# Row blocks of a mixture-of-experts layer rounded up to multiples of 16

## The chip, the cores and the metric

The kernel runs on one core of a Trainium2 chip. The metric is the device time of one execution in microseconds (us); the time of a kernel is the median of several runs.

## The reference

One layer of a hybrid encoder, for 1024 tokens of width 1024: a token mixer, and then a mixture of experts, which is where the change lies. Cut to that:

```python
logits = hf @ router_w + router_b                     # 32 experts
top_logits, top_idx = lax.top_k(logits, 4)
gates = softmax(top_logits)
...
def expert(xb, e):
    up = xb @ w_up[e] + b_up[e]                       # 1024 -> 2048
    x_glu, x_lin = split(up, 2)
    x_glu = minimum(x_glu, 7.0); x_lin = clip(x_lin, -7.0, 7.0)
    act = x_glu * sigmoid(1.702 * x_glu) * (x_lin + 1.0)
    return act @ w_down[e] + b_down[e]                # 1024 -> 1024
...
y[t] = sum over the 4 experts of gates[t, k] * expert(h[t], top_idx[t, k])
out = rms_norm(x + g2 * y, final_norm_w)
```

Each token's result is the gated sum over its four experts; a row that is added with a value of zero changes nothing.

## The kernel before, in words

Until about 585 us the token mixer and the router run. They leave in HBM the normalised tokens `h2s` (1024 rows of 2048 float16 values: high and low halves of each number), the residual `acc_d` (1024 float32 rows) to which the experts add, and a table `idtab`, which holds for each expert the list of its tokens (row number and gate). The 128 rows behind row 1024 of `h2s`, `acc_d` and `out` are zeros, and unused entries of the table point at them.

Then 32 experts follow. They are ranked by their load, and the expert of rank r is given room for `CAPS[r]` tokens (210, 192, 182 down to 108). `ORDER` pairs a small one with a large one: ranks 29, 0, 28, 1, 27, 2 and so on, and at the end 30 and 31. For an expert with room for n tokens (class `Expert`, L1699):

- The list is cut into blocks of up to 128 rows (`self.rows`, L1703): 210 becomes 128 + 82, 114 stays one block of 114. There are 52 blocks with 4522 rows in all.
- `load_ids` (L1714) reads a block's piece of the table. `gather` (L1726) has GpSimd (POOL) fetch the block's rows of `h2s` into the tile `xr` by an indirect DMA. `turn_x` (L1734) transposes them on TensorE (PE) into `xT`, with ScalarE copying out of PSUM.
- Three kinds of phases follow: G and L (the two halves of the up projection) and D (the down projection). Experts with more than 170 rows have them in halves. In a phase PE multiplies 128x128 pieces of weights, each three times (high and low halves), by all n columns (L1787 to L1789).
- The weights come as float32 in pieces of 512 KB into 14 buffers `wf`, by DMAs that SP issues (L1766). ScalarE and VectorE split each piece into float16 halves `wh` and `wl` (L1886, L1887), up to six pieces ahead of the matmuls.
- What a phase leaves in PSUM is worked on during the next phase, in slots between its matmuls (`epilogue`). For G that is a clamp on VectorE, a sigmoid on ScalarE and a product on POOL (L1810, the gate product). For D, `y_pieces` (L1848) has ScalarE write `yT` (feature by token, one buffer), PE transposes it back block by block (L1872), ScalarE scales by the gates into `yr` (L1873), and POOL adds the rows to `acc_d` by an indirect DMA that accumulates (L1875). That scatter waits for the landing of the scatter before it.

So the work of POOL is in program order: gate products, table pieces, gathers for the expert two places later (slot 5 of a phase), scatters. The last expert does not scatter: `LastRows.gather` and `finish` (L1960, L1966) fetch its rows of `acc_d`, add, normalise and write them to `out`, after `FinalNorm` has loaded, normalised (the pairs L1948 and L1949 on POOL) and stored all other rows.

Of the kernel before, what the change touches and what calls it, by code (L numbers as in the profile page):

```python
# [11 lines left out]
F32 = mybir.dt.float32  # L12
# [3 lines left out]
AF = mybir.ActivationFunctionType  # L16
# [107 lines left out]
def build(ctx, tc, A, out, dbg=None):  # L124
    nc = tc.nc
    V, S, G, PE, SY = nc.vector, nc.scalar, nc.gpsimd, nc.tensor, nc.sync
# [8 lines left out]
    def pst(shape=(128, 512), dt=F32, tag="g"):  # L135
        return ps.tile(list(shape), dt, name=f"ps_{tag}", bufs=BANKS[tag])
# [11 lines left out]
    id16 = cst.tile([128, 128], F16, name="id16")  # L148
# [105 lines left out]
    for r0, src in ((0, A["b_mod"]), (48, A["c"]), (56, A["norm1_w"]), (64, A["norm2_w"])):  # L254
        n = src.shape[1] // 128
# [62 lines left out]
    p = pst(tag="o")  # L318
# [909 lines left out]
    for i in range(-1, NT):  # L1228
        h = i + 1
        n = 2 if left["s5"] else 1  # L1230
# [358 lines left out]
    t, b, i = NT - 3, NT - 2, NT - 1  # L1589
# [36 lines left out]
    mx = mctx.enter_context(tc.tile_pool(name="mx", bufs=2))  # L1626

    def tpt(shape=(128, 512), dt=F32):
        return tpp.tile(list(shape), dt, name="tp")
# [3 lines left out]
    with tc.manual_schedule():  # L1633
# [6 lines left out]
        p = tpt()  # L1640
# [15 lines left out]
        p = tpt()  # L1656
# [15 lines left out]
        g2s = mc.tile([128, 8], F32, name="g2s")  # L1672
# [26 lines left out]
    class Expert:  # L1699
        def __init__(self, n, e, row, bias, q, tail=False):  # L1700
            self.n, self.get_e, self.get_row, self.bias, self.q = n, e, row, bias, q
            self.eid = None
            self.rows = [(0, min(n, 128))] + ([(128, n - 128)] if n > 128 else [])  # L1703
            self.per = 512 // n
            every, lo, hi = list(range(8)), [0, 1, 2, 3], [4, 5, 6, 7]
            fits = 3 * self.per >= 8
            self.down = [every] if fits else [lo, hi]
            if fits and not tail:
                self.up = [[("G", every)], [("L", every)]]
            else:  # L1710
                self.up = [[("G", lo), ("L", lo)], [("G", hi), ("L", hi)]]
            self.xT = self.aT = self.yT = self.glu = self.final = None

        def load_ids(self, after=(), q=None):  # L1714
            self.ids = []
            q = q or self.q
            row = self.get_row(q)
            for j, (r0, c) in enumerate(self.rows):
                t = mx.tile([c, 2], I32, name=f"ids{j}", bufs=7)
                ld = q.dma_start(t, idtab[ds(row + r0, c), :])  # L1720
                for s in after:
                    tc.add_manual_dep(ld.ins, s.ins.name, mybir.DependencyInfo(mybir.DependencyClass.Sync, mybir.DependencyReason.DATA),
                                      reason="every entry of the table")
                self.ids.append(t)

        def gather(self):  # L1726
            self.xr = []
            for j, (r0, c) in enumerate(self.rows):
                x = mx.tile([c, 2 * D], F16, name=f"xr{j}", bufs=2)
                G.indirect_dma_start(out=x, out_offset=None, in_=h2s[:, :],  # L1730
                                     in_offset=bass.IndirectOffsetOnAxis(ap=self.ids[j][:, 0:1], axis=0))
                self.xr.append(x)

        def turn_x(self):  # L1734
            def piece(j, q):
                r0, c = self.rows[j]
                if self.xT is None:
                    self.xT = mx.tile([128, 16, self.n], F16, name="xT")
                p = tpt((128, 8, c), F16)
                for k in range(8):  # L1740
                    kk_ = q * 8 + k
                    PE.transpose(p[:, k, :], self.xr[j][:, kk_ * 128:(kk_ + 1) * 128], id16[0:c, 0:c])  # L1742
                S.copy(self.xT[:, q * 8:q * 8 + 8, r0:r0 + c], p)  # L1743

            return [(0 + 2 * j + q, lambda j=j, q=q: piece(j, q)) for j in range(len(self.rows)) for q in range(2)]
# [6 lines left out]
    class Phase:  # L1752
# [95 lines left out]
        def y_pieces(self):  # L1848
            x = self.x
            if x.yT is None:  # L1850
                x.yT = mx.tile([128, 8, x.n], F32, name="yT", bufs=1)

            def evac(q):
                for i, m in enumerate(self.ms):
                    b = i // x.per
                    if b // 2 != q:
                        continue
                    S.activation(x.yT[:, m, :], self.loc(i), AF.Identity, scale=g2s[:, m:m + 1], bias=x.bias(16 + m))  # L1858

            ps_ = [(q, lambda q=q: evac(q)) for q in range(2)]  # L1860
            if self.ms[-1] != 7:
                return ps_
            yr = {}

            def rows(j, q):
                r0, c = x.rows[j]
                if q == 0:
                    yr[j] = mx.tile([c, D], F32, name=f"yr{j}", bufs=1)
                y = yr[j]
                p = tpt()  # L1870
                for m in range(4):
                    PE.transpose(p[0:c, m * 128:(m + 1) * 128], x.yT[:, q * 4 + m, r0:r0 + c], ident)  # L1872
                S.activation(y[:, q * 512:(q + 1) * 512], p[0:c, :], AF.Copy, scale=x.ids[j][:, 1:2].bitcast(F32))  # L1873
                if q == 1:
                    G.indirect_dma_start(out=acc_d[:, :],  # L1875
                                         out_offset=bass.IndirectOffsetOnAxis(ap=x.ids[j][:, 0:1], axis=0),
                                         in_=y, in_offset=None, compute_op=ADD)

            if x.final:
                return ps_ + [(3, lambda: x.final(x))]  # L1880
            return ps_ + [(3 + 2 * j + q, lambda j=j, q=q: rows(j, q)) for j in range(len(x.rows)) for q in range(2)]

    def split_w(w):
# [73 lines left out]
    class LastRows:  # L1957


        def gather(self, x):  # L1960
            c = x.n
            self.x = stg.tile([128, D], F32, name="wf")[0:c, :]
            G.indirect_dma_start(out=self.x, out_offset=None, in_=acc_d[:, :],
                                 in_offset=bass.IndirectOffsetOnAxis(ap=x.ids[0][:, 0:1], axis=0))

        def finish(self, x):  # L1966
            c = x.n
            ids = x.ids[0]
            z = stg.tile([128, D], F32, name="wf")[0:c, :]
            junk = mx.tile([128, D], F32, name="yr1", bufs=1)  # L1970
            y = self.y = mx.tile([c, D], F32, name="ly", bufs=1)
            ss = mx.tile([128, 2], F32, name="ls", bufs=1)[0:c, :]
            for q in range(2):
                p = tpt()
                cs = slice(q * 512, (q + 1) * 512)
                for m in range(4):
                    PE.transpose(p[0:c, m * 128:(m + 1) * 128], x.yT[:, q * 4 + m, :], ident)
                V.scalar_tensor_tensor(y[:, cs], p[0:c, :], ids[:, 1:2].bitcast(F32), self.x[:, cs], op0=MULT, op1=ADD)
                S.activation(junk[0:c, cs], y[:, cs], AF.Square, accum_out=ss[:, q:q + 1])
            G.tensor_scalar(ss[:, 0:1], ss[:, 0:1], 1.0 / D, EPS, op0=MULT, op1=ADD)  # L1980
            G.tensor_scalar(ss[:, 0:1], ss[:, 1:2], 1.0 / D, ss[:, 0:1], op0=MULT, op1=ADD)
            G.tensor_tensor(ss[:, 0:1], ss[:, 0:1], mhalf[0:c, 0:1], op=OP.pow)
            for q in range(2):
                cs = slice(q * 512, (q + 1) * 512)
                V.scalar_tensor_tensor(z[:, cs], y[:, cs], ss[:, 0:1], fw[0:c, cs], op0=MULT, op1=MULT)
            G.indirect_dma_start(out=out[:, :], out_offset=bass.IndirectOffsetOnAxis(ap=ids[:, 0:1], axis=0),
                                 in_=z, in_offset=None)
# [46 lines left out]
    with tc.If(over > 0):  # L2034
# [15 lines left out]
        for q in range(4):  # L2050
            p = tpt()
# [5 lines left out]
        p = tpt()  # L2057
# [5 lines left out]
        with tc.For_i(0, over, 1) as bi:  # L2063
# [5 lines left out]
            x = Expert(128, lambda: e, lambda q: row, lambda m: bt[:, m:m + 1], SY, True)  # L2069
# [37 lines left out]
```

## Time and profile before

| | |
|---|---|
| time, median of 3 runs | 1909.22 us (1908.97 to 1916.93) |
| the profiled execution | 1911.87 us, its span 1910.2 us |
| PE busy | 1753.9 us, 92% of the span |
| VectorE (DVE) busy | 1583.3 us, 83% |
| ScalarE (ACT) busy | 1236.3 us, 65% |
| GpSimd (POOL) busy | 575.1 us, 30% |
| indirect gathers L1730, scatters L1875 | 52 and 51 |

The profile is one execution. PE's matmuls overlap, so that its busy time says that it has work, not that it is at its peak. "Clock" is the share of full speed that TensorE was granted. A wait is put down to what ended last before the waiting instruction could start. "Us to landing" of a DMA runs from its issue to the time at which its last data has arrived.

### The profile page before, as it was taken

To read this page: it belongs to the slowest core of one execution; us is meant where nothing else is said; L and a number is where in the kernel's file an instruction comes from. 1 tells how busy PE (TensorE), PEld (TensorE's weight loads), DVE (VectorE), ACT (ScalarE), POOL (GpSimd) and SP (SyncE) were. 2 spreads that over 40 slices of the span, in tenths; PEclk is the share of its full clock that TensorE was granted. 3 is DMA by queue.
4 is the path that set the end of the run, shared out by engine and by line. 5 is a ranking of instruction groups with operands and counts; after the bars stand their busy time and mean duration, and the time that the engine had idled before them with its cause. 6 is when DMAs were issued, how large, how long until landed. Compare 5 with 4: busy or idle time off the path is not lost.

```text
span 1910.2 us, 57330 instructions
## 1 busy us (share of the span) xinstructions
PE 1753.9 (92%) x23174; PEld 1559.7 (82%) x23174; DVE 1583.3 (83%) x2430; ACT 1236.3 (65%) x1714; POOL 575.1 (30%) x505
## 2 busy tenths in 40 slices
PE   6889988999974999999999989999999999999983
PEld 3756665556643899999999979999999999999973
DVE  7858677765576888888897969999999999999985
ACT  2722333212234777777787868888888888888874
POOL 3834110143434223132221413213133333233214
PEclk9989999999996999999999989999999999999997
DMA  8841246632229999999998989999999999999996
GB/s 293 285 103 39 59 148 201 215 128 71 72 81 287 335 317 288 355 327 336 329 346 285 365 268 380 368 367 372 361 371 355 366 365 341 369 374 354 364 327 206
DMA packets 189451, 533.54 MB, mean 279 GB/s; under 512 B 37710, under 2 KB 47880, under 8 KB 189148
## 3 DMA queue, kind: packets, MB, share of 16 engines
q1 hardware_dynamic: 167548, 490.92, 71.6%
q0 software_dynamic: 21344, 37.85, 8.3%
q8 instruction: 183, 3.00, 0.6%
q10 hardware_dynamic: 288, 1.05, 0.1%
q14 instruction: 88, 0.72, 0.1%
HBM read 489.81 MB, written 39.30 MB: 277 GB/s over the span
## 4 chain that ended last, share of the span: by engine, by line
PE 46%; DMA 12%; ACT 4%; DVE 3%; issue 3%; POOL 1%; SPq 0%; DVEq 0%; ACTq 0%; POOLq 0%
PE ac L1787 14%; PE ac L1788 14%; PE ac L1789 14%; DMA wf<-in_w_up_dram 10%; ACT wh L1886 3%; DVE wl L1887 2%; PE tp L1872 2%; PE tp L1742 2%; DMA wf<-in_w_down_dram 2%; DMA xr<-h2s,ids 1%; ACT yT L1858 1%; POOL fs L1948 0%; ACT yr L1873 0%; DMA idtab<-pairs,dest 0%; POOL fs L1949 0%
## 5 line engine op out<-in xcount | busy, mean ns | idle before, releaser
L1887 DVE SCALAR_TENSOR_TENSOR wl<-wf,wh 128x1024 f16<-128x1024 f32 x768 | 944.5, 1270 | 137.3 <-ACT wh L1886 127.5
L1886 ACT ACTIVATE wh<-wf 128x1024 f16<-128x1024 f32 x768 | 774.3, 1055 | 50.3 <-DMA wf<-in_w_up_dram 21.4
L1789 PE MATMUL ac<-xT,wl 128*128 128x122 f16 (+27 forms) x4096 | 770.3, 226 | 4.5 <-DVE wl L1887 4.5
L1787 PE MATMUL ac<-xT,wh 128*128 128x122 f16 (+27 forms) x4096 | 770.9, 226 | 3.2 <-DVE el L1826 1.4
L1788 PE MATMUL ac<-xT,wh 128*128 128x122 f16 (+27 forms) x4096 | 770.4, 226 | 0.6 <-ACT xT L1743 0.6
L1789 PEld LDWEIGHTS <-wl 128*128 128x128 f16 x6144 | 602.2, 98 | 10.9 <-DVE wl L1887 8.8
L1788 PEld LDWEIGHTS <-wh 128*128 128x128 f16 x6144 | 603.4, 98 | 5.5 <-issue 4.1
L1787 PEld LDWEIGHTS <-wh 128*128 128x128 f16 x6144 | 602.9, 98 | 5.5 <-ACT wh L1886 3.6
L1787 PE MATMUL ac<-aT,wh 128*128 128x122 f16 (+27 forms) x2048 | 380.0, 226 | 3.1 <-DVE eg L1804 2.0
L1789 PE MATMUL ac<-aT,wl 128*128 128x122 f16 (+27 forms) x2048 | 380.0, 225 | 1.8 <-DVE wl L1887 1.7
L1788 PE MATMUL ac<-aT,wh 128*128 128x122 f16 (+27 forms) x2048 | 380.0, 225 | 0.9 <-DVE aT L1840 0.9
L1875 POOL DMA_INDIRECT acc_d<-yr,ids x51 | 135.2, 2651 | 592.2 <-ACT yr L1873 409.0
L1810 POOL TENSOR_TENSOR eg<-eg,es 128x420 f32<-128x420 f32 (+28 forms) x74 | 102.5, 1385 | 301.7 <-ACT es L1809 301.7
L1858 ACT ACTIVATE yT<-ac,BALL,g2s 128x122 f32<-128x122 f32 (+27 forms) x256 | 97.7, 473 | 9.1 <-PE ac L1789 9.1
L1837 ACT ACTIVATE aT<-el 128x420 f16<-128x420 f32 (+28 forms) x74 | 45.2, 611 | 90.2 <-DVE el L1830 89.3
L1743 ACT COPY xT<-tp 128x1024 f16<-128x1024 f16 (+27 forms) x104 | 75.8, 730 | 29.9 <-PE tp L1742 29.5
L1730 POOL DMA_INDIRECT xr<-h2s,ids x52 | 85.7, 1647 | 30.8 <-issue 19.7
L1809 ACT ACTIVATE es<-eg 128x420 f32<-128x420 f32 (+28 forms) x74 | 44.8, 605 | 74.3 <-DVE eg L1804 72.2
L1742 PE MATMUL tp<-id,xr 128*128 128x128 f16 (+27 forms) x832 | 54.3, 204 | 29.6 <-DMA wf<-in_w_up_dram 22.8
L1872 PE MATMUL tp<-C,yT 128*128 128x128 f32 (+27 forms) x408 | 68.4, 281 | 13.4 <-ACT yT L1858 10.1
L1826 DVE TENSOR_SCALAR el<-ac,BALL 128x122 f32<-128x122 f32 (+27 forms) x256 | 75.9, 355 | 0.0
L1804 DVE TENSOR_SCALAR eg<-ac,BALL 128x122 f32<-128x122 f32 (+27 forms) x256 | 74.8, 355 | 0.0
(495 smaller groups left out, 2426.0 us busy)
## 6 DMA issues: line engine op xcount, KB each, us to landing
wf<-in_w_up_dram SPq DMA_DIRECT2D x512, 512.0 KB, 8.4
wf<-in_w_down_dram SPq DMA_DIRECT2D x256, 512.0 KB, 10.0
wst<-in_w_mod_dram SPq DMA_DIRECT2D x40, 512.0 KB, 4.4
wst<-in_w_in_dram SPq DMA_DIRECT2D x16, 576.0 KB, 5.5
x<-in_x_dram SPq DMA_DIRECT2D x16, 512.0 KB, 4.4
hTb<-hT_d SPq DMA_DIRECT2D x16, 512.0 KB, 5.4
wA<-in_w_mod_dram SPq DMA_DIRECT2D x8, 512.0 KB, 10.3
hT_d<-hTa SPq DMA_DIRECT2D x8, 512.0 KB, 5.5
```

The costliest lines, as they stand in the source:

```text
L1730: G.indirect_dma_start(out=x, out_offset=None, in_=h2s[:, :], in_offset=bass.IndirectOffsetOnAxis(ap=self.ids[j][:, 0:1], axis=0))
L1742: PE.transpose(p[:, k, :], self.xr[j][:, kk_ * 128:(kk_ + 1) * 128], id16[0:c, 0:c])
L1787: PE.matmul(dst, h[:, ms], xh, start=k == 0 and m % x.per == 0, stop=False, skip_group_check=True)
L1788: PE.matmul(dst, h[:, ms], xl, start=False, stop=False, skip_group_check=True)
L1789: PE.matmul(dst, l[:, ms], xh, start=False, stop=k == 7, skip_group_check=True)
L1810: G.tensor_tensor(g, g, s, op=MULT)
L1826: V.tensor_scalar(t[i][:, q, :], self.loc(i + q), x.bias(8 + m), 8.0 * SS, op0=ADD, op1=MIN)
L1858: S.activation(x.yT[:, m, :], self.loc(i), AF.Identity, scale=g2s[:, m:m + 1], bias=x.bias(16 + m))
L1872: PE.transpose(p[0:c, m * 128:(m + 1) * 128], x.yT[:, q * 4 + m, r0:r0 + c], ident)
L1875: G.indirect_dma_start(out=acc_d[:, :], out_offset=bass.IndirectOffsetOnAxis(ap=x.ids[j][:, 0:1], axis=0), in_=y, in_offset=None, compute_ ...
L1886: S.activation(h, w, AF.Copy, scale=SW)
L1887: V.scalar_tensor_tensor(l, w, SW, h, op0=MULT, op1=SUB)
```

## The change

`self.rows` becomes a list of triples: first row, rows c, and c rounded up to a multiple of 16. The table pieces, the gathered tile `xr`, the row tile `yr` and the scatter use the rounded number; the transposes into `xT` and all matmuls still use c. `yT` becomes as wide as the first row of the last block plus its rounded rows (`wide`), and where this is more than n, POOL sets the added columns to zero before the evacuation. The transposes back then give zero rows for the added places, and the scatter adds those. An added entry is either an unused one, which points at the zero rows, or the token of an expert with more tokens than its room; such tokens are worked on in the loop for the overflow, as before. The last expert's gather and final rows are widened from 108 to 112.

```diff
--- before.py
+++ after.py
@@ -1700,7 +1700,9 @@
         def __init__(self, n, e, row, bias, q, tail=False):
             self.n, self.get_e, self.get_row, self.bias, self.q = n, e, row, bias, q
             self.eid = None
-            self.rows = [(0, min(n, 128))] + ([(128, n - 128)] if n > 128 else [])
+            cuts = [(0, min(n, 128))] + ([(128, n - 128)] if n > 128 else [])
+            self.rows = [(r0, c, -(-c // 16) * 16) for r0, c in cuts]
+            self.wide = self.rows[-1][0] + self.rows[-1][2]
             self.per = 512 // n
             every, lo, hi = list(range(8)), [0, 1, 2, 3], [4, 5, 6, 7]
             fits = 3 * self.per >= 8
@@ -1715,7 +1717,7 @@
             self.ids = []
             q = q or self.q
             row = self.get_row(q)
-            for j, (r0, c) in enumerate(self.rows):
+            for j, (r0, _, c) in enumerate(self.rows):
                 t = mx.tile([c, 2], I32, name=f"ids{j}", bufs=7)
                 ld = q.dma_start(t, idtab[ds(row + r0, c), :])
                 for s in after:
@@ -1725,7 +1727,7 @@
 
         def gather(self):
             self.xr = []
-            for j, (r0, c) in enumerate(self.rows):
+            for j, (_, _, c) in enumerate(self.rows):
                 x = mx.tile([c, 2 * D], F16, name=f"xr{j}", bufs=2)
                 G.indirect_dma_start(out=x, out_offset=None, in_=h2s[:, :],
                                      in_offset=bass.IndirectOffsetOnAxis(ap=self.ids[j][:, 0:1], axis=0))
@@ -1733,13 +1735,13 @@
 
         def turn_x(self):
             def piece(j, q):
-                r0, c = self.rows[j]
+                r0, c, _ = self.rows[j]
                 if self.xT is None:
                     self.xT = mx.tile([128, 16, self.n], F16, name="xT")
                 p = tpt((128, 8, c), F16)
                 for k in range(8):
                     kk_ = q * 8 + k
-                    PE.transpose(p[:, k, :], self.xr[j][:, kk_ * 128:(kk_ + 1) * 128], id16[0:c, 0:c])
+                    PE.transpose(p[:, k, :], self.xr[j][0:c, kk_ * 128:(kk_ + 1) * 128], id16[0:c, 0:c])
                 S.copy(self.xT[:, q * 8:q * 8 + 8, r0:r0 + c], p)
 
             return [(0 + 2 * j + q, lambda j=j, q=q: piece(j, q)) for j in range(len(self.rows)) for q in range(2)]
@@ -1848,14 +1850,16 @@
         def y_pieces(self):
             x = self.x
             if x.yT is None:
-                x.yT = mx.tile([128, 8, x.n], F32, name="yT", bufs=1)
+                x.yT = mx.tile([128, 8, x.wide], F32, name="yT", bufs=1)
+                if x.wide > x.n:
+                    G.memset(x.yT[:, :, x.n:x.wide], 0.0)
 
             def evac(q):
                 for i, m in enumerate(self.ms):
                     b = i // x.per
                     if b // 2 != q:
                         continue
-                    S.activation(x.yT[:, m, :], self.loc(i), AF.Identity, scale=g2s[:, m:m + 1], bias=x.bias(16 + m))
+                    S.activation(x.yT[:, m, 0:x.n], self.loc(i), AF.Identity, scale=g2s[:, m:m + 1], bias=x.bias(16 + m))
 
             ps_ = [(q, lambda q=q: evac(q)) for q in range(2)]
             if self.ms[-1] != 7:
@@ -1863,7 +1867,7 @@
             yr = {}
 
             def rows(j, q):
-                r0, c = x.rows[j]
+                r0, _, c = x.rows[j]
                 if q == 0:
                     yr[j] = mx.tile([c, D], F32, name=f"yr{j}", bufs=1)
                 y = yr[j]
@@ -1958,13 +1962,13 @@
 
 
         def gather(self, x):
-            c = x.n
+            c = x.wide
             self.x = stg.tile([128, D], F32, name="wf")[0:c, :]
             G.indirect_dma_start(out=self.x, out_offset=None, in_=acc_d[:, :],
                                  in_offset=bass.IndirectOffsetOnAxis(ap=x.ids[0][:, 0:1], axis=0))
 
         def finish(self, x):
-            c = x.n
+            c = x.wide
             ids = x.ids[0]
             z = stg.tile([128, D], F32, name="wf")[0:c, :]
             junk = mx.tile([128, D], F32, name="yr1", bufs=1)
```

Three places in POOL's order. First the start of the experts, where the second expert in the order (rank 0, 128 + 82 rows) and the third (rank 28, 114 rows) get their tokens; `ids` is a piece of the table. Before:

```order
L1720 DMA ids_5952<-idtab 128x2
L1720 ISA
L1720 DMA ids_5954<-idtab 82x2
L1730 DMA xr_5956<-h2s,ids_5952 128x2048
L1730 DMA xr_5958<-h2s,ids_5954 82x2048
L1931 TENSOR_LOAD ordi
L1931 ISA x2
L1720 ISA
L1720 DMA ids_5969<-idtab 114x2
```

Now:

```order
L1722 DMA ids_5952<-idtab 128x2
L1722 ISA
L1722 DMA ids_5954<-idtab 96x2
L1732 DMA xr_5956<-h2s,ids_5952 128x2048
L1732 DMA xr_5958<-h2s,ids_5954 96x2048
L1935 TENSOR_LOAD ordi
L1935 ISA x2
L1722 ISA
L1722 DMA ids_5969<-idtab 128x2
```

The order is the same; the second gather has 96 rows and the third expert's list 128.

Second, the place where the expert of rank 24 (122 rows in one block) is scattered; `eg` is the gate product of the expert after it. Before:

```order
L1810 TENSOR_TENSOR eg<-eg,es 128x656 x2
L1875 DMA acc_d<-yr_15801,ids_11863 1152x1024
L1931 TENSOR_LOAD ordi
L1931 ISA x2
L1720 ISA
L1720 DMA ids_16192<-idtab 128x2
L1720 ISA
L1720 DMA ids_16194<-idtab 30x2
L1730 DMA xr_16196<-h2s,ids_15349 126x2048
```

Now:

```order
L1812 TENSOR_TENSOR eg<-eg,es 128x656 x2
L1855 MEMSET yT 128x8x6
L1879 DMA acc_d<-yr_15810,ids_11867 1152x1024
L1935 TENSOR_LOAD ordi
L1935 ISA x2
L1722 ISA
L1722 DMA ids_16201<-idtab 128x2
L1722 ISA
L1722 DMA ids_16203<-idtab 32x2
L1732 DMA xr_16205<-h2s,ids_15357 128x2048
```

The memset of 6 columns for each of the 8 pieces of features stands between the gate product and the scatter. The scatter itself names the whole of `acc_d`; its rows are those of `yr`, 128 now.

Third, the tail, where POOL works out the norms `fs` of the 8 stored tiles and then that of the last expert's rows, `ls`. The first row is the end of the sixth pair. Before:

```order
L1949 TENSOR_TENSOR fs_33101<-fs_33101,mhalf_72 128x1
L1948 TENSOR_SCALAR fs_33141<-fs_33141 128x1
L1949 TENSOR_TENSOR fs_33141<-fs_33141,mhalf_72 128x1
L1948 TENSOR_SCALAR fs_33148<-fs_33148 128x1
L1949 TENSOR_TENSOR fs_33148<-fs_33148,mhalf_72 128x1
L1980 TENSOR_SCALAR ls_33157<-ls_33157 108x1
```

Now:

```order
L1953 TENSOR_TENSOR fs_33127<-fs_33127,mhalf_72 128x1
L1855 MEMSET yT_33157 128x8x4
L1952 TENSOR_SCALAR fs_33168<-fs_33168 128x1
L1953 TENSOR_TENSOR fs_33168<-fs_33168,mhalf_72 128x1
L1952 TENSOR_SCALAR fs_33175<-fs_33175 128x1
L1953 TENSOR_TENSOR fs_33175<-fs_33175,mhalf_72 128x1
L1984 TENSOR_SCALAR ls_33184<-ls_33184 112x1
```

The last memset stands behind six pairs and ahead of two. The eight transposes of the last expert (L1977 before) wait for ScalarE's `yT`, and now the first of them for this memset as well.

## Rows read from the trace of the kernel before

**Rows 1.** Windows: busy us (instructions) by engine, clock, DMA share, GB/s.

```profile
core 0: us, PE busy (x) PEld busy (x) DVE busy (x) ACT busy (x) POOL busy (x), PEclk, DMA share, GB/s
639.30:646.10 6.80, 5.12 (x37) 4.63 (x38) 3.39 (x6) 3.03 (x5) 1.07 (x1) 0.50 1.04 378
1124.00:1134.20 10.20, 7.08 (x64) 5.99 (x62) 5.48 (x5) 6.30 (x7) 1.76 (x1) 0.50 0.60 187
1160.00:1200.00 40.00, 40.00 (x665) 39.71 (x663) 38.45 (x47) 33.56 (x44) 10.96 (x8) 1.00 1.03 383
```

**Rows 2.** SP's waits, 1040:1160 first, then 1320:1480: total, times, longest.

```profile
SPq L1766 <- DMA wf<-in_w_up_dram: 42.6, 43, 3.8
SPq L1766 <- DVE wl L1887: 100.0, 99, 2.5
```

**Rows 3.** PE's waits, 585 to 650: total us, times, longest.

```profile
PE tp L1742 <- DMA xr<-h2s,ids: 6.3, 2, 4.5
```

**Rows 4.** PE's waits, 1042 to 1053.

```profile
PE tp L1872 <- ACT yT L1858: 2.5, 2, 2.2
PE tp L1872 <- ACT yr L1873: 0.9, 1, 0.9
```

**Rows 5.** Chain that ended last: start us, us, link; three stretches.

```profile
625.93 15.01 DMA xr<-h2s,ids
...
1017.93 25.50 DMA wf<-in_w_up_dram
...
1097.81 30.94 DMA wf<-in_w_up_dram
```

**Rows 6.** PE's waits, 1119 to 1142.

```profile
PE ac L1789 <- DVE wl L1887: 2.7, 3, 0.9
PE ac L1787 <- ACT wh L1886: 2.5, 3, 1.1
PE tp L1872 <- ACT yr L1873: 0.8, 1, 0.8
```

**Rows 7.** Scatters issued at 727.9, 896.4, 1054.0, 1091.6: us to landing.

```profile
acc_d<-yr,ids POOLq DMA_INDIRECT x1, 22.0
...
acc_d<-yr,ids POOLq DMA_INDIRECT x1, 7.6
...
acc_d<-yr,ids POOLq DMA_INDIRECT x1, 10.3
...
acc_d<-yr,ids POOLq DMA_INDIRECT x1, 34.9
```

**Rows 8.** Gathers issued at 598.2, 599.5, 737.8: us to landing (128, 82, 128 rows).

```profile
xr<-h2s,ids POOLq DMA_INDIRECT x1, 7.6
...
xr<-h2s,ids POOLq DMA_INDIRECT x1, 20.5
...
xr<-h2s,ids POOLq DMA_INDIRECT x1, 15.1
```

**Rows 9.** PE's waits, 680 to 940.

```profile
PE tp L1872 <- ACT yT L1858: 4.9, 3, 1.7
```

**Rows 10.** The page, part 3: software DMA queue, packets, MB, share of 16 engines.

```profile
q0 software_dynamic: 21344, 37.85, 8.3%
```

**Rows 11.** Groups kept apart by shape, ScalarE, L1873: busy us, mean ns.

```profile
L1873 ACT ACTIVATE yr<-tp,ids 122x512 f32<-122x512 f32 x4 | 2.8, 707 | 0.5 <-PE tp L1872 0.5
L1873 ACT ACTIVATE yr<-tp,ids 8x512 f32<-8x512 f32 x4 | 2.7, 666 | 0.2 <-PE tp L1872 0.2
```

**Rows 12.** Groups kept apart by shape, POOL: a memset.

```profile
L877 POOL MEMSET ke<- 128x256 f32 x2 | 0.6, 302 | 0.0
```

**Rows 13.** Timeline of the tail, one row of POOL, one of DVE: start, us.

```profile
1889.80 1.29 POOL L1948 TENSOR_SCALAR fs<-fs 128x1 f32<-128x1 f32 x1
...
1894.94 1.40 DVE L1978 SCALAR_TENSOR_TENSOR ly<-tp,ids,wf 108x512 f32<-108x512 f32 x2
```

**Rows 14.** The page, part 5: POOL's gate product.

```profile
L1810 POOL TENSOR_TENSOR eg<-eg,es 128x420 f32<-128x420 f32 (+28 forms) x74 | 102.5, 1385 | 301.7 <-ACT es L1809 301.7
```

## The prediction

> **What bounds the kernel now.** I read the windows first, then who waited for whom, then the chain, then the landing times of the indirect transfers.
>
> From 1160 us on the TensorE (PE) row is solid: in 1160:1200 PE is busy 40.00 of 40 us at clock 1.00, and the DMA engines move 383 GB/s [rows 1]. SP, which issues the weight loads, is then held back only by buffers that VectorE has not yet released (100.0 us in 99 waits in 1320:1480, [rows 2]); weights wait for the compute. A faster gather or scatter is worth nothing in that stretch.
>
> Before 1160 the reader should find three places. (1) At the start of the experts PE waited twice, 6.3 us in all, the longer time 4.5, for gathered rows `xr` [rows 3]. [...] (2) Around 1043 PE waited 2.5 and 0.9 us for ScalarE's evacuations [rows 4], while the chain shows a weight load that took 25.50 us, to 1043.43 [rows 5]. (3) Between 1119 and 1142 PE waited 2.7 and 2.5 us for split weights and 0.8 for an evacuation [rows 6]; the chain has a weight load of 30.94 us, to 1128.75 [rows 5], and from 1124 to 1134.2 the clock was 0.50, PE busy 7.08 us, and the DMA engines moved only 187 GB/s [rows 1].
>
> Why were those loads slow? The indirect transfers land very unevenly. The scatters of 54 and 128 rows landed after 7.6 and 10.3 us, those of 82 and 122 rows after 22.0 and 34.9 us [rows 7] (by the order of the blocks the issue at 727.9 has 82 rows, at 896.4 54, at 1054.0 128, at 1091.6 122). Among gathers, 128 rows took 7.6 us, and the 82 rows issued 1.3 us later 20.5 us [rows 8]. So it is not the number of rows that decides: 82 and 122 are 2x41 and 2x61, which no number from 3 to 16 divides; 54 is 6x9 and 128 is 16x8. That is what a split into equal shares looks like, over two DMA engines at worst. A weight load is spread over all of them and would be late when two hold 41 or 61 rows each. The 30.94 us load began at 1097.81, 6 us after the 122-row scatter went out; the 25.50 us load follows the scatter of the other expert with 122 rows.
>
> [...]
>
> **The change part by part.** Every block becomes 16, 32, 48, 64, 96, 112 or 128 rows. The nearest rows for the new blocks are those of 128: 7.6 and 15.1 us for a gather, 10.3 us for a scatter [rows 7, 8].
>
> *A, the start.* The 82-row gather (96 now) went out at 599.5 and landed at 620.0; at 7.6 to 15.1 us it lands by 615, before PE wants it (1.8 us ahead of 620.0), so that wait of 6.3 - 4.5 = 1.8 us goes. The 114-row gather (128 now) went out at 625.93 and took 15.01 us [rows 5], so PE had come for it at about 636.5; without the first wait it comes at 634.7. On POOL this gather stands behind two gate products whose input ScalarE makes after it has copied the transposes of those 82 rows, so it goes out 1.8 us sooner, at 624.1, and lands at 632 to 639. The wait becomes 0 to 4.5 us; I take 1.0, nearer the 7.6, the row closest in time. So 6.3 - 1.0 = 5.3 us. With so short a wait I expect no half clock, and half of 5.12 us, 2.6, comes back. A = 7.9 us (1.8 if the long wait and its clock stay, 8.9 if all goes).
>
> *B, around 1043:* both waits go, 2.5 + 0.9 = 3.4 us.
>
> *C, 1119 to 1142:* 2.7 + 2.5 + 0.8 = 6.0 us, and half of the 7.08 us at half clock, 3.5. C = 9.5 us. Next to be late after B and C would be the DMA engines as a whole; 383 GB/s in 1160:1200 against 187 says that they have room.
>
> *What stays:* three waits for `yT` between 680 and 940, 4.9 us [rows 9]. There ScalarE has weight splits ahead of the evacuation in its own order, and the change does not touch that.
>
> *Rows added.* 4522 rows become 4736: 214 more, each gathered and scattered. The software queue took 8.3% of 16 engines' span [rows 10], 158.5 us, or 0.035 us a row, so 214 rows make 7.5 us of all engines. In the solid stretch this hides behind SP's waits for VectorE [rows 2]. The 22 rows of the last four experts I count as on the path, 0.8 us. The 98 rows of the first fifteen experts would cost 3.4 us if the DMA engines paced them; I take 0, since the same transfers get shorter there, and keep 3.4 for the bound.
>
> *Work of the engines.* Transposes, copies and products keep their free sizes and only their partitions grow. A copy `yr` takes 707 ns with 122 partitions and 666 with 8 [rows 11]: at most 0.05 us a copy, on a ScalarE that PE does not wait for in the solid stretch. I take 0. If it were all on the path, 102 copies would make 5 us.
>
> *The memsets.* POOL gets 27. One of 256 elements a partition took 302 ns [rows 12]; these have 16 to 112, so up to 0.3 us each. 26 of them stand behind a gate product of the phase before and ahead of the scatter, which itself waits for the transposes that read the padded tile, so POOL reaches them early: 0. Without that cover, 26 x 0.3 = 8 us. The 27th is in the tail, behind six of the eight norm pairs, so that the last transposes start only near 1890; VectorE reads them at 1894.94, after its last store [rows 13], which covers them. But the two norm pairs behind the memset are on the chain. Bounds: 0, and 1.29 us, which a one-column operation took there while VectorE ran [rows 13]; I take 0.2, because the operation behind it would otherwise have had that wait itself.
>
> *Sum:* 7.9 + 3.4 + 9.5 - 0.8 - 0.2 = 19.8 us saved. The profiled execution took 1911.87 us (span 1910.2), so it would take 1892.1; it lies 2.65 us above the median of the runs shown, 1909.22, from which I get 1889.4, say **1889 us**. Its own bounds: A at 1.8, 4.2 us for rows and 1.3 in the tail leave 9.2 saved (1900); A at 8.9 and nothing paid gives 21.8 (1887).
>
> **The rivals.**
>
> *More comes back.* The three `yT` waits go too, because ScalarE no longer starts its splits late, and with them some clock. For it: such waits are missing after 1160. Against: it is ScalarE's own order. 19.8 + 4.9 = 24.7, and 30.9 if the 1.0 of A and two spells like A's 2.6 are added: 1878 to 1885.
>
> *The weights still pace it.* The DMA engines cannot deliver faster and B and C return as waits for other loads. For it: SP waited 42.6 us for earlier up-projection loads in 1040:1160 [rows 2]. Against: 383 GB/s right after. Then A alone is left, less 3.4 and 1.0: 3.5 us saved, 1906.
>
> *The change does not do what it says.* If all 16 engines already took every indirect transfer, nothing is redistributed, and the added rows and memsets are paid: 1 to 5.5 us, 1910 to 1915. [...] Against it: 20.5 beside 7.6 us [rows 8].
>
> *Slower.* POOL becomes the gate: a memset waits in POOL's order behind a late gate product, and the last block's transposes, which now wait for POOL, hold PE. It costs from the point at which the memset ends after the last evacuation to `yT`. At that product's mean of 1385 ns [rows 14] 26 times make 36 us, against 20 saved: 1925. Against it: POOL is busy for 30% of the span, and the product belongs to the phase before.
>
> **How the numbers follow.** Forecast 0.55, more comes back 0.20, weights still pace 0.15, no redistribution 0.07, slower 0.03. A change under 0.5%, 9.5 us, can hardly be told from none here; that is 1899.7 to 1918.8. Faster by more than that: the forecast nearly whole, the first rival and a little of the second, 0.77. Within: the rest of the second, the third and a little of the others, 0.19. Slower: 0.04. For 8 in 10 I take 1877 to 1903: the forecast's 1887 to 1900, the first rival, and the nearer part of the second.
>
> **What would show it.** Right: landing times of the indirect transfers all between 6 and 16 us; no weight load above some 20 us on the chain between 1000 and 1140; PE's waits for `xr` near 1 us in all; no half clock around 1124; the stretch after 1160 as solid as before, only begun earlier. Wrong: scatters of the former 122-row blocks still above 20 us; PE waiting for POOL at the transposes of `yT`; weight loads near 30 us although every scatter lands in 10; a tail that is more than 1 us longer.

## The result and the profile after

The changed kernel takes **1893.45 us**, the median of 8 runs (1889.28 to 1902.9), beside 1910.24 us for the kernel before in 8 runs of the same chip: a ratio of **0.9909 [0.9891, 0.9928]**, 16.8 us by the medians. Forecast were 1889 us and 19.8 us. The profiled execution was the fastest of the eight, 1889.28 us, and the one profiled before lay 1.6 us above its median, so that the span is 22.7 us shorter and not 16.8. Lines behind `self.rows` are numbered 2 to 4 higher than before (L1742 is now L1744, L1872 is L1876, L1766 is L1768).

The page of the changed kernel, parts 1, 3 and 4:

```profile
span 1887.5 us, 57403 instructions
PE 1743.0 (92%) x23174; PEld 1554.1 (82%) x23174; DVE 1581.3 (84%) x2430; ACT 1234.9 (65%) x1714; POOL 576.0 (31%) x532
...
q0 software_dynamic: 14144, 39.57, 8.6%
...
PE 54%; DMA 6%; ACT 3%; issue 3%; DVE 2%; POOL 1%; DVEq 0%; POOLq 0%; SPq 0%; ACTq 0%
```

The engines are as busy as before. The software queue moved 4.5% more bytes in a third fewer packets [rows 10]. On the chain DMAs have 6% now; before, the page had 12%:

```profile
PE 46%; DMA 12%; ACT 4%; DVE 3%; issue 3%; POOL 1%; SPq 0%; DVEq 0%; ACTq 0%; POOLq 0%
```

*The start.* PE's waits, 585 to 680 (total us, times, longest), the wait ahead of the first expert left out (24.4 us, before 22.8):

```profile
PE tp L1876 <- ACT yT L1862: 1.3, 1, 1.3
PE ac L1791 <- DVE wl L1891: 1.0, 2, 0.7
PE tp L1744 <- ACT xT L1745: 0.9, 1, 0.9
```

The two waits for `xr` [rows 3] are gone. But the waits for `yT` and `wl` are new: before, PE had neither in this stretch.

*The middle.* Windows of the changed kernel: busy us (instructions) by engine, clock, DMA share, GB/s:

```profile
639.30:646.10 6.80, 6.80 (x79) 6.80 (x77) 5.04 (x8) 5.18 (x8) 1.50 (x2) 1.00 0.92 297
...
1040.00:1060.00 20.00, 20.00 (x307) 19.94 (x305) 19.03 (x25) 17.14 (x21) 8.68 (x4) 1.00 1.02 359
...
1124.00:1140.00 16.00, 16.00 (x250) 16.00 (x248) 16.00 (x26) 11.49 (x14) 8.86 (x4) 1.00 1.03 351
1160.00:1200.00 40.00, 40.00 (x659) 39.61 (x657) 36.66 (x45) 34.02 (x46) 4.66 (x4) 1.00 0.99 358
```

What [rows 1] show after 1160 now begins at 1000. PE has no wait at all between 1000 and 1160, the clock stays at 1.00, and the DMA engines move 351 GB/s around 1130 instead of 187. The chain in 1000 to 1160, by line, holds only matmuls and transposes where it had loads of 25.50 and 30.94 us [rows 5]:

```profile
by line: PE ac L1789 31.4%; PE ac L1790 31.1%; PE ac L1791 31.1%; PE tp L1876 3.6%; PE tp L1744 2.9%
```

And SP, in 1040 to 1160, waits for the split and no longer for earlier loads [rows 2]:

```profile
SPq L1768 <- DVE wl L1891: 72.6, 73, 2.6
```

*The landings.* In this trace no landing of a gather or scatter is resolved. In a second profiled execution of the changed kernel (below, "the change again") 40 are, and they took 5.6 to 11.4 us; those resolved before took 6.0 to 35.6. The scatter of the first block that had 122 rows, issued at 1003.6 there (us to landing):

```profile
acc_d<-yr,ids POOLq DMA_INDIRECT x1, 9.9
```

*What stayed.* PE's waits, 680 to 940, beside [rows 9]:

```profile
PE tp L1876 <- ACT yT L1862: 5.1, 3, 1.8
PE ac L1791 <- DVE wl L1891: 0.9, 2, 0.5
```

*The tail.* From the last expert matmul to the end of the span it is 29.8 us, before 29.6. Timelines of POOL and of DVE in the tail (start, us):

```profile
1867.10 0.12 POOL L1855 MEMSET yT<- 128x32 f32 x1
...
1869.23 1.29 POOL L1952 TENSOR_SCALAR fs<-fs 128x1 f32<-128x1 f32 x1
```

```profile
1871.17 1.28 DVE L1958 SCALAR_TENSOR_TENSOR wf<-wf,fs,fw 128x1024 f32<-128x1024 f32 x1 [0.71 <-POOL fs L1953]
1872.38 1.40 DVE L1982 SCALAR_TENSOR_TENSOR ly<-tp,ids,wf 112x512 f32<-112x512 f32 x2
```

PE waits 9.5 us there, by the waits for this memset, but VectorE reads the transposes right behind its last store. So that wait costs nothing, as in [rows 13].

### The profile page after: what moved, and what is told of

Its sections match the earlier page's. It is cut to its first block, busy times and chain, and to the rows that moved or that the text cites. A ratio compares the mean times of both kernels' runs of the same rounds, so it can differ in the third digit from the quotient of the medians.

```text
span 1887.5 us, 57403 instructions
## 1 busy us (share of the span) xinstructions
PE 1743.0 (92%) x23174; PEld 1554.1 (82%) x23174; DVE 1581.3 (84%) x2430; ACT 1234.9 (65%) x1714; POOL 576.0 (31%) x532
## 3 DMA queue, kind: packets, MB, share of 16 engines
q0 software_dynamic: 14144, 39.57, 8.6%
## 4 chain that ended last, share of the span: by engine, by line
PE 54%; DMA 6%; ACT 3%; issue 3%; DVE 2%; POOL 1%; DVEq 0%; POOLq 0%; SPq 0%; ACTq 0%
PE ac L1789 17%; PE ac L1791 17%; PE ac L1790 16%; DMA wf<-in_w_up_dram 4%; PE tp L1876 2%; ACT wh L1890 2%; PE tp L1744 2%; DVE wl L1891 2%; DMA wf<-in_w_down_dram 1%; POOL fs L1952 0%; DMA ids<-idtab 0%; ACT yT L1862 0%; DVE el L1828 0%; DMA fw<-in_final_norm_w_dram 0%; DMA idtab<-pairs,dest 0%
## 5 line engine op out<-in xcount | busy, mean ns | idle before, releaser
L1879 POOL DMA_INDIRECT acc_d<-yr,ids x51 | 129.0, 2530 | 569.0 <-ACT yr L1877 388.7
L1812 POOL TENSOR_TENSOR eg<-eg,es 128x420 f32<-128x420 f32 (+28 forms) x74 | 108.5, 1466 | 301.7 <-ACT es L1811 300.8
L1732 POOL DMA_INDIRECT xr<-h2s,ids x52 | 84.8, 1630 | 32.1 <-issue 10.9
L1744 PE MATMUL tp<-id,xr 128*128 128x128 f16 (+27 forms) x832 | 53.4, 201 | 25.3 <-DMA ids<-idtab 24.4
L1876 PE MATMUL tp<-C,yT 128*128 128x128 f32 (+6 forms) x408 | 65.8, 278 | 10.3 <-ACT yT L1862 9.0
```

The lines of the kernel that those rows point to most:

```text
L1744: PE.transpose(p[:, k, :], self.xr[j][0:c, kk_ * 128:(kk_ + 1) * 128], id16[0:c, 0:c])
L1812: G.tensor_tensor(g, g, s, op=MULT)
L1879: G.indirect_dma_start(out=acc_d[:, :], out_offset=bass.IndirectOffsetOnAxis(ap=x.ids[j][:, 0:1], axis=0), in_=y, in_offset=None, compute_ ...
```

## The experiments

Two theories stood against each other. **Shares:** a transfer is cut into equal shares for its DMA engines, at most the 16 that the profile counts, which is a guess from the landing times [rows 7, 8]. A block whose rows divide badly then sits on few of them, and weight loads, whose queue had 103.7% of 16 engines' time in 639.3 to 646.1 of the kernel before, come late; the two blocks of 122 rows carry the gain around 1043 and 1130, and the 82- and 114-row gathers the gain at the start. **Sum:** every rounded block brings a little, by its packets or in another way. Two narrower ones stand in the expectations: that the gathers alone matter, and that the small packets do. The diffs are against the changed kernel. The "expert stretch" is the time from the first transpose of `xr` to the end of the last expert matmul (before 1282.3 us, changed kernel 1258.0).

### The gathers alone, the scatters alone, the tables alone

Gathers alone: the tables and gathers take the rounded rows, scatters and `yT` the old ones (with `x.ids[j]` cut to `c` rows there), and there is no memset.

```diff
-            self.wide = self.rows[-1][0] + self.rows[-1][2]
+            self.wide = n
...
-                r0, _, c = x.rows[j]
+                r0, c, _ = x.rows[j]
```

> Table pieces and gathers have rounded rows, the scatter has the old counts and no memset. Shares theory (a transfer runs on as many DMA engines as the largest divisor of its rows up to 16, and a scatter of 122 rows on two engines delays the weight loads): only the start comes back, A of 8 us, so 7 to 9 us faster than before; the scatters issued near 1001 and 1079 still land after about 35 us, the waits around 1040 and 1120 (3.4 and 6.0 us, and the half clock) are there again. Gather theory (those two places came from late gathers and late tables, which only stood beside the scatters): 17 to 22 us faster, and no wait there.

Scatters alone: tables, scatters and memsets as in the change, gathers as before.

```diff
-            for j, (_, _, c) in enumerate(self.rows):
+            for j, (_, c, _) in enumerate(self.rows):
```

> Table pieces and scatters have rounded rows, the gathers the old counts. Shares theory: B and C come back, 11 to 13 us faster than before; PE waits for gathered rows at the start as before, 6.3 us. The gathers of 122 and 124 rows keep landing after 25 us and more, and if they too delay weight loads some part of B and C stays. Gather theory: about 0 to 2 us faster.

Tables alone: both edits together.

> Only the table pieces are read in rounded rows; gathers and scatters are as before. Shares theory: within 2 us of before, since a table piece is 8 bytes a row. Count theory (what the change saves are the thousands of small packets of the software queue, 8 bytes each, which stand between the weight packets): the number of packets under 512 bytes falls as it did with the whole change, from 37710 to about 30100, and most of the 17 us comes with it.

Measured against the kernel before (1912.39 us, 23 runs): gathers 1906.23 us, 0.9973 [0.9962, 0.9985]; scatters 1898.41 us, 0.9928 [0.9908, 0.9948]; tables 1912.03 us, 0.9995 [0.9984, 1.0006], with the 21344 software packets of before. So the tables bring nothing, the gathers some 5 us (2 below what was expected), the scatters some 14 (1 above; 9.9 to 17.6 by the interval). That the gathers alone matter is refuted. The small packets did not fall with the tables, so this run says nothing on whether they are what makes the transfers late. With the gathers alone PE's waits in 1030 to 1150 read:

```profile
PE tp L1876 <- ACT yT L1862: 6.3, 1, 6.3
PE tp L1876 <- ACT yr L1877: 1.3, 1, 1.3
```

The start is mended and the middle is not. With the scatters alone it is the other way round: 4.2 us of waits for `xr` at the start and no wait in 1030 to 1150.

### Only the two blocks of 122 rows, and their scatters alone

```diff
-            self.rows = [(r0, c, -(-c // 16) * 16) for r0, c in cuts]
+            self.rows = [(r0, c, 128 if n == 122 else c) for r0, c in cuts]
```

> The kernel before with the two blocks of 122 rows alone rounded to 128, in table, gather and scatter; 50 blocks as before. Shares theory: B and C come back and A does not, 10 to 13 us faster than before; the waits of 3.4 and 6.0 us near 1043 and 1120 are gone, those of 6.3 us at the start stay. If it is the sum of all small unevennesses that matters, 2 blocks of 52 give less than 4 us.

The same with their gathers left at 122 rows (the edit of "scatters alone" added):

> The kernel before, with the token tables of the two blocks of 122 rows rounded to 128 and only their scatters taking 128 rows; their gathers take 122 as before, and nothing else is rounded. Shares theory with the scatters as the cost: nearly all that rounding these two blocks whole brought, 10 to 20 us below the kernel before (ratio 0.990 to 0.995), with no wait of PE left between 1119 and 1142. Rival (the gathers of these two blocks cost as much, since a gather of 122 rows has the same two shares of 61): about half, 5 to 10 us, with waits of PE for xr of those two experts or weight loads of over 15 us left behind their gathers.

Both blocks whole: 1892.66 us, 0.9892 [0.9873, 0.9911], 20 us less than the kernel before, as much as all 27 blocks together (ratios 0.9909, 0.9899 and 0.9919 in three measurements) and more than either theory expected of it. Their scatters alone: 1898.51 us beside 1913.71 us of the kernel before (23 runs), 0.9924 [0.9901, 0.9946], 15 us. PE's waits of the second, 600 to 680 and then 940 to 1160:

```profile
PE tp L1744 <- DMA xr<-h2s,ids: 5.0, 2, 4.2
...
PE tp L1876 <- ACT yr L1877: 0.3, 1, 0.3
```

Two scatters out of 103 indirect transfers make most of the difference, and the start is left as it was. The changed kernel measured beside this one took 1898.49 us, the same. The 5 us between the two kernels (their gathers) are not settled, since the intervals overlap.

### All but the two blocks of 122 rows

```diff
-            self.rows = [(r0, c, -(-c // 16) * 16) for r0, c in cuts]
+            self.rows = [(r0, c, c if n == 122 else -(-c // 16) * 16) for r0, c in cuts]
```

> The whole change, except that the two blocks of 122 rows stay at 122. Shares theory (a block whose count divides badly loads a few DMA engines and delays the weight loads spread over all of them): only the start is gained, as in the gathers alone, so 5 to 8 us below the kernel before (ratio 0.996 to 0.997), 10 to 15 us above the changed kernel; the scatter of 122 rows again lands after some 35 us, PE waits again near 1043 and near 1120 to 1140 with half clock there, and weight loads of 20 us or more are back on the chain. Rival (the gain is a sum over all 27 rounded blocks): 17 x 25/27, some 16 us below the kernel before, and no weight load over 20 us on the chain.

> The changed kernel again, as the one that the three others of this call are compared with: 1889 to 1898 us, ratio 0.988 to 0.993 of the kernel before.

1905.39 us, 0.9964 [0.9951, 0.9978], 8 us less than the kernel before; the changed kernel measured beside it took 1898.49 us, 0.9919 [0.9892, 0.9947]. The 7 us between the two are fewer than the 10 to 15 that were expected. Long loads are back on the chain (start, us, link), and so are PE's waits in 1030 to 1150:

```profile
1023.40 21.86 DMA wf<-in_w_up_dram
...
1105.37 26.24 DMA wf<-in_w_up_dram
```

```profile
PE tp L1876 <- ACT yT L1862: 6.5, 3, 5.7
PE tp L1876 <- ACT yr L1877: 1.7, 1, 1.7
```

Twenty-five rounded blocks with 202 of the 214 added rows brought what the start brings, and the middle came back with the two blocks that were left out. That speaks for shares and against the sum. (Landing times are not resolved in this trace, nor in those of the gathers, scatters or tables alone, so those parts of the expectations stay untested.)

### One row more or less: 126 and 127

The sharpest test of the shares: the blocks of 122 rows become 126 (14x9) or 127 (a prime) in place of 128.

```diff
-            self.rows = [(r0, c, -(-c // 16) * 16) for r0, c in cuts]
+            self.rows = [(r0, c, 127 if n == 122 else -(-c // 16) * 16) for r0, c in cuts]
```

> The changed kernel, but the two blocks of 122 rows become 126, which is 14 times 9, and not 128. Shares theory: 14 engines with 9 rows each are as good as 16 with 8; within 2 us of the changed kernel (about 1890 to 1893), no wait of PE near 1040 and 1120. If whole multiples of 16 are needed: as slow there as with 122, 10 to 13 us slower than the changed kernel.

> One row more than the last: the two blocks become 127 rows, a prime number. Shares theory: all 127 rows on one engine, 127 x 0.29 us (34.9 us for 61 rows before, less what it waits for) or more, so scatters that take 50 to 75 us; the weight loads beside them wait, and PE loses more than before at those places: 10 to 40 us each, so 1905 to 1950. If the number of rows or the multiple of 2 decides: like 126.

126 rows: **1892.61 us**, 0.9899 [0.9865, 0.9932] of the kernel before. 127 rows: **1969.45 us**, 1.0302 [1.027, 1.0334]. One row more in two blocks costs 77 us and turns the gain into a loss of 55, more than the shares theory expected (1905 to 1950 us). The scatter issued at 1082.6 with 126 rows, and the one at 1132.9 with 127 (us to landing):

```profile
acc_d<-yr,ids POOLq DMA_INDIRECT x1, 10.9
```

```profile
acc_d<-yr,ids POOLq DMA_INDIRECT x1, 66.5
```

Three more rows of the 127-row kernel: on its chain the other 127-row gather; among ScalarE's waits the copy to `yr`, a single buffer, for the scatter before it to land; and its window 1060 to 1100, in which PE has little to do:

```profile
940.16 46.67 DMA xr<-h2s,ids
```

```profile
ACT yr L1877 <- DMA acc_d<-yr,ids: 30.2, 1, 30.2
```

```profile
1060.00:1100.00 40.00, 10.23 (x132) 9.65 (x130) 8.01 (x7) 8.52 (x12) 1.94 (x1) 0.62 0.44 130
```

With 126 rows PE is busy 40.00 of these 40 us. So a multiple of 16 is not needed: 126 rows, 14 times 9, took 1892.61 us, where the changed kernel measured beside it (128 rows; the next section) took 1893.42.

### Seven blocks in place of 27, and the change again

Only blocks of 46, 82, 114, 116, 122 (two) and 124 rows are rounded.

```diff
-            self.rows = [(r0, c, -(-c // 16) * 16) for r0, c in cuts]
+            self.rows = [(r0, c, -(-c // 16) * 16 if c in (46, 82, 114, 116, 122, 124) else c) for r0, c in cuts]
```

> Only the seven blocks with 46, 82, 114, 116, 122, 122 and 124 rows are rounded, those with 19 rows and more for each engine by the shares theory; the other 45 blocks keep their counts. 7 memsets and 64 added rows instead of 27 and 214, and none in the tail. Shares theory: as fast as the changed kernel or up to 1 us faster (1889 to 1893). If the small blocks of the second half matter too: 2 us or more slower than it.

> The changed kernel once more, beside the others on one chip: 1889 to 1903 us as in the first measurement, whose runs spread over 14 us where those of before spread over 8. If the spread comes from weight loads that are now and then late, a slower run has a lower mean clock and PE waits before 1160; otherwise the time is lost outside the experts.

1893.9 us, 0.9904 [0.9881, 0.9928], and 1893.42 us, 0.9899 [0.9873, 0.9925]. The seven blocks add 58 rows (the 64 of the expectation is a slip). The other 20 roundings, their rows and memsets give nothing and cost nothing that can be measured.

### The waits that stayed

The three waits for `yT` were put down, by the order of the work, to ScalarE standing at a half of the activated product whose input VectorE has not made yet. In this kernel both halves come one slot later.

```diff
-                for at, f in ((0, lin), (1, prod), (2, high), (2, low)):
+                for at, f in ((0, lin), (1, prod), (3, high), (3, low)):
```

> The changed kernel, with the two halves (high and low) of the activated gate product made one slot of the phase's order later. If the three waits for yT (1.60 + 1.71 + 1.82 us in the changed kernel's profile near 747, 831 and 914, and their short companions) come from ScalarE standing in its own order at a half whose input VectorE has not made yet, they go: 3 to 8 us below the changed kernel, no wait of PE for yT between 740 and 920. If ScalarE is only late as a whole, the waits stay or turn up at the product that reads the halves: 0 to 5 us slower.

1908.2 us, 0.9977 [0.9961, 0.9993]: some 10 us slower than the changed kernel measured beside it, where 3 to 8 us less, or 0 to 5 us more, were expected. The waits did go. PE has none between 680 and 940, and its clock stays at 1.00 from 612.6 to 1855.1. But in 1160 to 1780, where the changed kernel's PE waits for nothing, it now has these waits, and the window 1400 to 1600 falls from 200.00 us busy to:

```profile
PE ac L1791 <- DVE wl L1891: 7.6, 10, 1.2
PE tp L1876 <- ACT yr L1877: 4.6, 6, 0.8
```

```profile
1400.00:1600.00 200.00, 195.63 (x3125) 190.12 (x3123) 179.65 (x223) 164.04 (x222) 82.36 (x41) 1.00 0.98 353
```

ScalarE's own waits in that window show what it stands at instead, first in this kernel, then in the changed kernel:

```profile
ACT es L1811 <- DVE eg L1806: 15.0, 5, 3.9
ACT es L1811 <- POOL eg L1812: 12.8, 4, 4.1
```

```profile
ACT es L1811 <- DVE eg L1806: 11.7, 6, 2.3
```

It now stands at the sigmoid for up to 4.1 us, VectorE's split stands behind ScalarE's (waits of DVE for `wh` 19.1 us, in the changed kernel 8.9), and the later experts pay more than the early ones gain. The order of ScalarE's work is not all of it. On POOL the scatters' instructions took 4551 ns each in place of 2530 (part 5 of the two pages, changed kernel first):

```profile
L1879 POOL DMA_INDIRECT acc_d<-yr,ids x51 | 129.0, 2530 | 569.0 <-ACT yr L1877 388.7
```

```profile
L1879 POOL DMA_INDIRECT acc_d<-yr,ids x51 | 232.1, 4551 | 551.8 <-ACT yr L1877 373.8
```

The longest wait for POOL, which ended at 1454.26, came behind one such scatter of 10.11 us, issued at 1437.49, two gathers and then the late gate product. Why the scatters hold POOL longer here is open, and so is how much of the 10 us is theirs. The later slots for the early experts alone were not tried.

## Why the prediction was right, and which terms were not

Faster was right, the time of 1893.45 us lies 4 us above the forecast, and the mechanism is the one that was argued. Its signs of being right came: landing times of 5.6 to 11.4 us where they are resolved (6 to 16 was named), no load above 20 us on the chain between 1000 and 1140, no wait for `xr` (1 us was named), no half clock around 1124.

**Few engines for badly divisible blocks.** Shown: 126 against 127 rows (10.9 and 66.5 us to landing), and in the last section the packet counts and the 1.5 engines that the end of a 122-row scatter kept busy. "No redistribution" is refuted by it.

**The 25.50 and 30.94 us loads follow the two 122-row scatters.** Shown from both sides: without these two blocks the loads and waits stay, with their scatters alone both go. B and C (3.4 and 9.5 us, 12.9 in all) measured 15 us with the two scatters alone (10 to 19 by the interval). "The weights still pace it" is refuted: no load is late between 1000 and 1160 any more.

**A, the start, 7.9 us, was too large.** The gathers alone measure 5.2 us (0.0027 x 1912.4; 2.9 to 7.3 by the interval). The prediction counted what `xr` cost and not what lay under it. Its 2.6 us of clock are an estimate, half of the 5.12 us that PE was busy at 0.50 [rows 1]; that window has 1.00 now. PE's waits in 585 to 680, without the first, fell from 7.7 us (the 6.3 of [rows 3] and 1.4 of short ones) to 4.1 in the trace, 3.6 and not 5.3. The waits for `wl` and `yT` at 655 to 661 follow the pattern of the three that stayed in 680 to 940 ("wl" first, then "yT", one such place per pair of experts). In every kernel with the rounded 114-row gather they are there, the later halves apart; in those that keep the old gathers they are not. PE had come too late to meet them. The prediction said what would be late next behind B and C, but named nothing behind A. Nor do the terms simply add up: the two scatters alone (1898.51 us) and the whole change beside them (1898.49) took the same, so beside a mended middle A can't be told from nothing, though six runs each, which spread over 7 and 14 us, could hide some 5 us.

**What stays: right.** 4.9 us before, 5.1 now. "More comes back" needed these waits to go; they did not, and its time was not reached.

**The clock.** In the profiled execution the spells of half clock at 639.3 and 1124 are gone, as forecast, and two of 3.41 us in 680 to 940 besides, which were in no term of the sum ("more comes back" had them). That extra does not last: another profiled execution of the changed kernel has the same waits and half the clock behind each. Here is the row behind the first of the three waits, in the first execution and then, at the same place of the work, in the other:

```profile
748.40:751.80 3.40, 3.31 (x30) 2.81 (x31) 1.74 (x3) 3.40 (x9) 0.00 (x0) 1.00 1.02 393
```

```profile
755.20:758.60 3.40, 3.40 (x23) 3.14 (x21) 1.53 (x2) 3.40 (x6) 0.00 (x0) 0.50 1.05 392
```

Three profiled executions of the changed kernel have 2, 2 and 5 such spells in the expert stretch, which took 1258.0, 1259.0 and 1263.9 us. So a part of the gap between 22.7 us in the profile and 16.8 by the medians lies here. Among the eight runs of the result a mean clock of 0.967 or 0.968 goes with 1889.28 to 1891.75 us, one of 0.963 with 1900.68 and one of 0.962 with 1902.9. Late weight loads, which the expectation of "the change again" asked about, are not what is seen: the execution with five spells (1898.51 us) has no wait of PE between 940 and 1780 either.

**Rows added, memsets, tail.** Taken as 0.8, 0 and 0.2 us. The seven blocks measure the same as all 27, so rows and memsets cost nothing visible. The shortest memset took 111 ns and the longest 196 (mean of a shape), less than the 0.3 us of the bound; POOL is never what the transposes before the scatter wait for, which refutes the slower rival. The tail is 0.2 us longer.

**What the forecast did not see** is how concentrated the gain is: rounding two blocks of 52 was worth as much in the runs as rounding 27. The rows of before had it, since only the two 122-row blocks stand next to the late loads, but each block's share was never worked out. No version beats the changed kernel by more than the runs can tell; the one with the scatters of two blocks alone is the smallest that equals it.

## What to carry to other kernels

Before choosing the rows of an indirect transfer, measure what the neighbouring numbers cost: here scatters of 126 and 128 rows landed after 10.9 and 9.9 us, one of 122 after 34.9 and one of 127 after 66.5. Look for the harm in the loads that were issued shortly after as well (25.50 and 30.94 us here), and not only in the wait for the uneven transfer itself. When a stall is taken away, list the waits that the stalled engine would have met had it come earlier, as here, where the next ones of that kind stood in the trace a few places later.

## What the runs showed of the hardware

A scatter of 127 rows landed after 66.5 us and one of 126 after 10.9 us, in the same place of two kernels that differ only in that row; the gathers of 127 and 126 rows after 42.0 and 10.7 us. I had expected the prime to be bad, and not that two blocks would hold up everything for 77 us.

The number of packets of the software queue shows the uneven blocks without any landing time. It falls by 1696 when two 122-row scatters become 128 (19648 against 21344), by 3392 when the two gathers do so too (17952), which is 848 each, while the bytes hardly move (37.85, 37.88 and 37.93 MB); and it rises by 7552, four times 1888, when four transfers of 126 rows get 127 (14208 to 21760). Both differences fit equal shares, if a block's share is its rows divided by their largest divisor up to 16: 61 for 122 rows, 8 for 128, 127 for 127 and 9 for 126. And 16 x (61 - 8) = 848, 16 x (127 - 9) = 1888. Summed over all blocks, and the two transfers of the last expert's rows, this fit gives the differences between the kernels whose counts stand in this document to the packet: 7200 fewer in the changed kernel, as counted (14144 against 21344), where a limit of 15 or 18 in place of 16 would give 4464 or 6736.

Do these small packets or the unequal shares make the transfers late? The last 15 us of the 122-row scatter of [rows 7], which landed at 1126.5, tell. In 1110 to 1125 of the kernel before, and then in 1082 to 1092 of the changed kernel, where the same block's scatter has 128 rows and a gather runs beside it, the software queue had (packets, MB, share of 16 engines):

```profile
q0 software_dynamic: 75, 0.30, 9.5%
```

```profile
q0 software_dynamic: 350, 1.05, 39.4%
```

The 75 packets hold 4 KB on average, a row of the scatter each, and are the work of 1.5 engines of 16; the small ones have passed by then. So the end of this transfer is late by rows on few engines. What the small packets cost in its first 18 us is not shown.
